# A delta rule in chunks of 128 tokens instead of 64, with one state hand-over, an output norm moved forward and a router product turned round

## The chip, the cores and the metric

The kernel runs on one core of a Trainium2 chip. The metric is the time of one execution in device microseconds. The kernel before took 1208.31 us in the median of 3 runs (1206.81 to 1208.69).

## What is computed

One block of a model with 256 tokens of width 1024. A mixer has two halves: a gated delta rule with 4 heads of 128 (the part that is changed) and a banded attention with 8 heads of 64. Behind it follow an output projection, a router that picks 4 of 32 experts for each token, and the experts. Of the reference, the delta rule per chunk of tokens is:

```python
lower = einsum(k_beta, k) * decay * strict           # chunk x chunk, below the diagonal
tmat  = inverse(lower + eye)                         # triangular
u = tmat @ (v * beta);  w = tmat @ (k_beta * exp(g))
attn = einsum(q, k) * decay;  q_dec = q * exp(g);  k_dec = k * exp(g_last - g)
def step(state, ...):                                # chunk after chunk
    v_new = u - w @ state
    out   = q_dec @ state + attn @ v_new
    state = state * exp(g_last) + k_dec.T @ v_new
```

The reference takes chunks of 64 tokens, so 4 chunks. The result does not depend on the chunk length: with chunks of 128 there are 2 chunks, the first state is zero, and only one state is ever handed on.

The router computes logits = x @ w_router + b_router, takes the 4 largest, and the experts (1024 to 2048 to 1024, in fp32) are run in the order of their load. All 32 experts are read: 192 blocks of 2 MB.

## The kernel before, in words

**Memory.** Eight blocks of 16 KB per partition (`w0`, `w1`, `wA` to `wF`, line 65) and two more slots (`wh`, `wx`) are first weights and scratch of the mixer and later the ring in which expert weights are loaded (`RINGTAGS`, line 23). An expert load (line 1109, issued by SyncE, SP in the rows) waits until the mixer's last use of its slot. In the mixer `wE` and `wB` are the scratch of the delta rule, `w0` is the scratch of the attention and then free, and `wF` takes one block of adaLN weights after another (line 81, `modrow`, line 717: five of the later ones on VectorE, the others on TensorE).

**Order.** Lines 62 to 1036 are not run in written order: a planner places each instruction in its engine's queue (the DMA queue of SP too) by costs of its own, and work under `tc.high_priority()` goes first. `chain()` (line 487) is run under high priority (line 848), so the planner fills the gaps of the delta rule with products of `stream()` (line 407, all `mm3` at line 232), `attention()` (line 746) and `wout_b()` (line 816, the attention's half of the output projection). Lines 1037 to 1080 are a stretch in which TensorE and VectorE keep the written order: `wout_a` (the delta rule's half of the output projection), the residual, the router, the first gather.

**The delta rule, lines 524 to 712.** Tokens lie in two tiles `a` of 128, each with two chunks `e` of 64; a chunk takes 64 partitions.

- Lines 524 to 533: products of k with k and q for each chunk (line 531, 64 x 64 x 128).
- Lines 535 to 554: sums of the gates by matrices `tri` and `same` (lines 537 to 541) and their exponentials, among them the decay `egl` of each state.
- Lines 557 to 588: decay matrices `xL`, `xA` of 64 x 64 for 8 pairs (tile, head), and `L` = lower.
- Lines 592 to 654: the triangular inverse `U` by six levels of doubling. `pair_mm` (line 597) makes 16 products of 64 x 64 x 64, half of them on partitions 0 to 63 and half on 64 to 127. Each level has `xb`, `ub` and, but for the last, `tb`.
- Lines 659 to 675: u (line 667) and w (line 673), 16 products each.
- Lines 678 to 712: four steps. Each has w @ state (line 688), k_dec.T @ v_new into the new state (line 696, with the scaled sum on VectorE at line 702) and the output (lines 707 and 708, 128-row and 64-row products by turns).

An fp32 product is two MATMUL instructions in the trace; a transpose is one.

**Behind it.** `delta_out(a)` (line 882) is the output norm of tile a with the gate: squares on ScalarE (line 886), eleven small steps and four products on VectorE, four transposes (line 893). `split(...)` at line 867 puts the high part of the first half of `w_out` into `whx` (tag `acc`, the place of `kqT`), so it waits for the delta rule's last use of q. `logits` (line 931) multiplies with x as the stationary side (128 x 128) and 32 columns of router weights moving, 8 products for each tile, before `choice` (line 939) on VectorE.

Of the kernel before, what the change touches and what calls it, by code (L numbers as in the profile page):

```python
# [19 lines left out]
NEG = -1e30  # L20
# [29 lines left out]
def block_kernel(ctx, tc, x, small, rows, rel_ext, wpre, wexp, b_up, b_down, out,  # L50
# [214 lines left out]
    def late_constants():  # L265
        nonlocal ones, same, tri, id64, m_strict, m_incT, lvl, iot, iou, strib, strif, onesb, kadd_r, kadd_c, ecol, e96
        ones = const.tile([P, P], F32, name="ones")
        G.memset(ones, 1.0)

        same = const.tile([P, P], F32, name="same")  # L270
        G.memset(same, 0.0)
        G.memset(same[0:64, 0:64], 1.0)
        G.memset(same[64:128, 64:128], 1.0)
        tri = const.tile([P, P], F32, name="tri")
        V.scalar_tensor_tensor(tri, jp, 0.0, same, op0=ALU.is_ge, op1=ALU.mult)
# [6 lines left out]
        m_strict = const.tile([P, 64], F32, name="m_strict")  # L282
        V.tensor_scalar(m_strict, jl, 0.0, NEG, op0=ALU.is_ge, op1=ALU.mult)
        m_incT = const.tile([P, 64], F32, name="m_incT")
        V.tensor_scalar(m_incT, jl, 0.0, NEG, op0=ALU.is_lt, op1=ALU.mult)
# [29 lines left out]
        G.memset(onesb, 1.0)  # L315
        kadd_r = const.tile([96, NE], F32, name="kadd_r")
# [15 lines left out]
    ones = same = tri = id64 = m_strict = m_incT = lvl = iot = iou = strib = strif = onesb = None  # L332
    kadd_r = kadd_c = ecol = e96 = None
# [13 lines left out]
    vT, eq, kw, vbt = [fixed["wB"][0][:, 1024 * i:1024 * i + 1024].rearrange("p (h t) -> p h t", h=n_)  # L347
                       for i, n_ in enumerate((4, 4, 8, 8))]
# [138 lines left out]
    def chain():  # L487
# [36 lines left out]
        mps = []  # L524
        for a in range(2):
            mp = bank("dl")
            mv = mp.rearrange("p (h z t) -> p h z t", h=4, z=2)
            for h in range(4):
                for e in range(2):
                    c0 = a * 128 + e * 64  # L530
                    T.matmul(mv[64 * e:64 * e + 64, h], kqT[:, h, 0, c0:c0 + 64], kqT[:, h, :, c0:c0 + 64],
                             start=True, stop=True)
            mps.append(mp)
        yield 0.6
        sp = bank("dl")
        for a in range(2):
            T.matmul(sp[:, 4 * a:4 * a + 4], tri, g[:, a, :], start=True, stop=True)
            T.matmul(sp[:, 8 + 4 * a:12 + 4 * a], same, g[:, a, :], start=True, stop=True)
            for e in range(2):
                c_ = 16 + (2 * a + e) * 4  # L540
                T.matmul(sp[:, c_:c_ + 4], same[:, 64 * e:64 * e + 1].to_broadcast([P, P]), g[:, a, :],
                         start=True, stop=True)
        V.tensor_scalar(ln_, ln_, -0.5, None, op0=ALU.mult)
        aL, bb, aq, kd, ew = [const.tile([P, 8], F32, name=n_) for n_ in ("aL", "bb", "aq", "kd", "ew")]
# [3 lines left out]
        V.tensor_add(kd, bb, sp[:, 8:16])  # L548
        egl = const.tile([P, 4, 4], F32, name="egl")
        S.activation(ew, aL, AF.Exp)  # L550
        S.activation(kd, kd, AF.Exp)
        S.activation(egl.rearrange("p c h -> p (c h)"), sp[:, 16:32], AF.Exp)
        betaf = beta.rearrange("p a h -> p (a h)")
        V.tensor_mul(ew, ew, betaf)
        yield 0.8

        blE = block("wE")
        xL, xA, L, Ti, *Xs, aT, U = [blE[:, 512 * i:512 * i + 512].rearrange("p (c n) -> p c n", c=8) for i in range(8)]

        for a in range(2):  # L560
            mv = mps[a].rearrange("p (h z t) -> p h z t", h=4, z=2)
            S.copy(L[:, 4 * a:4 * a + 4, :], mv[:, :, 0, :])
            S.copy(aT[:, 4 * a:4 * a + 4, :], mv[:, :, 1, :])
        for a in range(2):
            bp = bank("dl")
            for h in range(4):
                T.transpose(bp[:, h * 128:(h + 1) * 128], bb[:, a * 4 + h:a * 4 + h + 1].to_broadcast([P, P]), ident)
            bpv = bp.rearrange("p (h t) -> p h t", h=4)
            for e in range(2):
                r_ = slice(64 * e, 64 * e + 64)  # L570
                V.tensor_add(xL[r_, 4 * a:4 * a + 4, :], bpv[r_, :, r_], m_strict[r_, None, :].to_broadcast([64, 4, 64]))
        V.tensor_add(xL, xL, aL[:, :, None].to_broadcast([P, 8, 64]))
        S.activation(xL, xL, AF.Exp)
        yield 0.6
        for a in range(2):
# [3 lines left out]
            apv = ap_.rearrange("p (h t) -> p h t", h=4)  # L579
            if a == 0:  # L580
                G.tensor_mul(xL, xL, betaf[:, :, None].to_broadcast([P, 8, 64]))
            S.activation(eq[:, :, a * 128:(a + 1) * 128], apv, AF.Exp)
            for e in range(2):
                r_ = slice(64 * e, 64 * e + 64)
                V.tensor_add(xA[r_, 4 * a:4 * a + 4, :], apv[r_, :, r_], m_incT[r_, None, :].to_broadcast([64, 4, 64]))
        yield 1.5
        for a in range(2):
            V.tensor_mul(L[:, 4 * a:4 * a + 4, :], L[:, 4 * a:4 * a + 4, :], xL[:, 4 * a:4 * a + 4, :])
        idb = id64[:, None, :].to_broadcast([P, 8, 64])
        H0, H1 = slice(0, 64), slice(64, 128)  # L590

        def level(s_):
            lm = k2("Lm", (P, 8, 64))
            (V if s_ < 2 else G).tensor_mul(lm, L, lvl[s_][:, None, :].to_broadcast([P, 8, 64]))
# [84 lines left out]
        for c in range(4):  # L679
# [30 lines left out]
            if c < 3:  # L710
                st = sn
# [684 lines left out]
```

## Time and profile before

| what | value |
|---|---|
| median of 3 runs | 1208.31 us (1206.81 to 1208.69) |
| the profiled execution | 1208.93 us, its span in the trace 1207.2 us |
| TensorE busy / VectorE / ScalarE / GpSimdE | 87% / 30% / 16% / 8% of the span |
| mean granted TensorE clock | 0.945 of 2.4 GHz |
| read from memory | 449.5 MB, of them 402.7 MB expert weights |

The profile has two stages. Up to about 270 us the mixer and the router run; from then on the experts. 1.73 us of the execution's time lie outside the span. A row of the timeline names start, length, engine, line, operation, result and operands (out<-in), the count of merged instructions, and in brackets the idle time ahead and who ended it.

### The profile page before, as it was taken

To read this page: it belongs to the slowest core of one execution; us is meant where nothing else is said; L and a number is where in the kernel's file an instruction comes from. 1 tells how busy PE (TensorE), PEld (TensorE's weight loads), DVE (VectorE), ACT (ScalarE), POOL (GpSimd) and SP (SyncE) were. 2 spreads that over 40 slices of the span, in tenths; PEclk is the share of its full clock that TensorE was granted. 3 is DMA by queue.
4 is the path that set the end of the run, shared out by engine and by line. 5 is a ranking of instruction groups with operands and counts; after the bars stand their busy time and mean duration, and the time that the engine had idled before them with its cause. 6 is when DMAs were issued, how large, how long until landed. Compare 5 with 4: busy or idle time off the path is not lost. (4 is left out here: it accounts for less than half of the span.)

```text
span 1207.2 us, 14829 instructions
## 1 busy us (share of the span) xinstructions
PE 1055.9 (87%) x5891; PEld 508.5 (42%) x5891; DVE 361.0 (30%) x852; ACT 190.2 (16%) x380; POOL 102.3 (8%) x93
## 2 busy tenths in 40 slices
PE   4799999999987889999985889999976699998995
PEld 2698997673431124334431233334421143333332
DVE  5488786763113012121211012122211011111113
ACT  3554115331100001010100001010100001010101
POOL 1547413200000000000000000000000000000001
PEclk9899798989998799999997899999998799999998
DMA  9925345697999999999999999999999999999994
GB/s 356 400 78 210 140 176 210 259 426 280 423 420 422 421 407 422 426 425 423 426 420 426 426 423 427 423 427 427 419 428 422 425 428 422 426 426 422 427 420 162
DMA packets 51464, 451.95 MB, mean 374 GB/s; under 512 B 5760, under 2 KB 7424, under 8 KB 9408
## 3 DMA queue, kind: packets, MB, share of 16 engines
q1 hardware_dynamic: 51392, 450.97, 90.1%
q8 instruction: 48, 0.79, 0.3%
q14 instruction: 24, 0.20, 0.0%
HBM read 449.50 MB, written 1.05 MB: 373 GB/s over the span
## 5 line engine op out<-in xcount | busy, mean ns | idle before, releaser
L1117 PE MATMUL dl<-w_f,xg 128*64 128x512 f32 (+1 forms) x224 | 110.7, 638 | 9.1 <-DMA w_f<-in_wexp_dram 9.1
L1171 DVE TENSOR_TENSOR acc<-acc,mm 128x512 f32<-128x512 f32 x52 | 35.8, 688 | 248.2 <-PE mm L1166 248.2
L1117 PE MATMUL mm<-w_f,xg 128*64 128x512 f32 (+2 forms) x208 | 93.9, 602 | 3.0 <-DMA w_f<-in_wexp_dram 3.0
L1273 POOL TENSOR_TENSOR wF_f<-acc,m_row 128x512 f32<-128x512 f32 x3 | 3.8, 1284 | 944.4 <-DVE acc L1171 944.4
L1117 PE MATMUL dl<-wh,xg 128*64 128x512 f32 (+2 forms) x144 | 68.4, 617 | 4.9 <-DMA wh<-in_wexp_dram 4.9
L1117 PE MATMUL dl<-wD_f,xg 128*64 128x512 f32 (+1 forms) x128 | 62.5, 638 | 4.4 <-DMA wD_f<-in_wexp_dram 4.4
L1166 PE MATMUL mm<-yg,wts 128*128 128x512 f32 x112 | 54.5, 614 | 9.9 <-ACT yg L1163 8.9
L1135 ACT ACTIVATE sg<-gm 128x512 f32<-128x512 f32 x28 | 17.6, 630 | 279.8 <-DVE gm L1133 255.5
L1117 PE MATMUL dl<-wE_f,xg 128*64 128x512 f32 (+2 forms) x112 | 53.0, 623 | 7.9 <-DMA wE_f<-in_wexp_dram 7.9
L1117 PE MATMUL mm<-wB_f,xg 128*64 128x512 f32 (+2 forms) x128 | 59.2, 609 | 0.0
L1117 PE MATMUL mm<-wh,xg 128*64 128x512 f32 (+1 forms) x144 | 56.8, 594 | 0.0
L998 PEld LDWEIGHTS tp<-oh,x 128*128 128x128 f32 x432 | 50.7, 192 | 13.2 <-issue 11.4
L1117 PE MATMUL dl<-wF_f,xg 128*64 128x512 f32 (+2 forms) x112 | 53.7, 620 | 2.3 <-DMA wF_f<-in_wexp_dram 2.3
L998 PE MATMUL tp<-oh,x 128*128 128x128 f32 x432 | 54.8, 279 | 0.7 <-ACT aT__3409 L1146 0.7
L1117 PE MATMUL dl<-wC_f,xg 128*64 128x512 f32 (+2 forms) x112 | 53.1, 616 | 1.8 <-DMA wC_f<-in_wexp_dram 1.8
L1117 PE MATMUL mm<-wE_f,xg 128*64 128x512 f32 (+1 forms) x112 | 51.3, 611 | 2.5 <-DMA wE_f<-in_wexp_dram 2.5
L1163 ACT COPY yg<-dl 128x512 f32<-128x512 f32 x27 | 15.8, 586 | 228.6 <-PE dl L1117 228.6
L1117 PE MATMUL mm<-wC_f,xg 128*64 128x512 f32 (+1 forms) x112 | 51.6, 611 | 0.0
L1008 DVE TENSOR_SCALAR xg<-tp,mc,mc 128x128 f32<-128x128 f32 x52 | 19.6, 406 | 103.4 <-PE dl L1117 94.7
L1117 PE MATMUL dl<-wB_f,xg 128*32 128x512 f32 (+1 forms) x96 | 46.8, 625 | 2.8 <-DMA wB_f<-in_wexp_dram 2.8
L1006 ACT ACTIVATE xg<-tp,mc,mc 128x128 f32<-128x128 f32 x52 | 21.9, 455 | 147.6 <-DVE xg L1008 147.6
L1117 PEld LDWEIGHTS mm<-w_f,xg 128*64 128x64 f32 (+2 forms) x208 | 28.0, 139 | 37.9 <-issue 32.1
(633 smaller groups left out, 2236.8 us busy)
## 6 DMA issues: line engine op xcount, KB each, us to landing
wh<-in_wexp_dram SPq DMA_DIRECT2D x57, 1024.0 KB, 25.0
w_f<-in_wexp_dram SPq DMA_DIRECT2D x26, 2048.0 KB, 26.0
wA_f<-in_wexp_dram SPq DMA_DIRECT2D x36, 1024.0 KB, 22.2
wF_f<-in_wexp_dram SPq DMA_DIRECT2D x36, 1024.0 KB, 29.7
wE_f<-in_wexp_dram SPq DMA_DIRECT2D x15, 2048.0 KB, 29.4
wC_f<-in_wexp_dram SPq DMA_DIRECT2D x15, 2048.0 KB, 27.0
wB_f<-in_wexp_dram SPq DMA_DIRECT2D x13, 2048.0 KB, 22.2
wD_f<-in_wexp_dram SPq DMA_DIRECT2D x13, 2048.0 KB, 34.2
```

The costliest lines, as they stand in the source:

```text
L998: T.matmul(b_[:, k * 128:(k + 1) * 128], x2[:, a, half(n)][:, k * 128:(k + 1) * 128], oh[:, a], start=a == tiles[0], stop=a == tiles[-1])
L1006: S.activation(xg[:, k], src, AF.Identity, scale=mc, bias=sc)
L1008: V.tensor_scalar(xg[:, k], src, mc, sc, op0=ALU.mult, op1=ALU.add)
L1117: T.matmul(b_[i * n:(i + 1) * n, :], lhs[:, k, i * n:(i + 1) * n], w(k), start=k == 0, stop=last and k == 7)
L1135: S.activation(sg, gm, AF.Sigmoid, scale=1.702)
L1163: S.copy(yg, b_)
L1166: T.matmul(cb, wt[:, a], yg, start=True, stop=True)
L1171: V.tensor_add(acc[:, a, sl], acc[:, a, sl], cb)
L1273: (V if a and n else G).tensor_mul(fin[:, 0, a, sl], acc[:, a, sl], m3_row[:, sl])
```

## The change

The chunk becomes 128 tokens, a whole tile. Products of k and q, decay matrices and `L` are 128 x 128 for each pair (tile, head). The inverse is still made for the 64 x 64 blocks on the diagonal (`Ld`, the same levels), and the block below the diagonal comes from one coupling step of 2 x 8 products of 64 x 64 x 64 with a copy behind each. u, w and the outputs are products of 128 x 128 x 128, and one state goes from tile 0 to tile 1; `egl` and the decayed sum of states go. PSUM copies of this part are cut in two, one half for ScalarE and one for VectorE. Beside it: `delta_out(0)` stands under high priority; `whx` is taken from block `w0` instead of tag `acc`; the router's product has 32 router columns as the stationary side in four column groups and 128 tokens moving, then a copy and one product with `stk` (four stacked 32 x 32 identities) that adds the four groups and turns the result. The diff, cut:

```diff
-        V.scalar_tensor_tensor(tri, jp, 0.0, same, op0=ALU.is_ge, op1=ALU.mult)
+        V.tensor_scalar(tri, jp, 0.0, None, op0=ALU.is_ge)
...
+        for i in range(4):
+            V.tensor_copy(stk[32 * i:32 * i + 32], ident[32 * i:32 * i + 32, 32 * i:32 * i + 32])
...
+        def products(z, a):
+            mp = bank("dl")
+            for h in range(4):
+                T.matmul(mp[:, h * 128:(h + 1) * 128], kqT[:, h, 0, a * 128:(a + 1) * 128], kqT[:, h, z, a * 128:(a + 1) * 128],
+                         start=True, stop=True)
+            mv = mp.rearrange("p (h t) -> p h t", h=4)
+            if z == 0:
+                V.tensor_mul(L[:, 4 * a:4 * a + 4], mv, betaf[:, 4 * a:4 * a + 4, None].to_broadcast([P, 4, P]))
+            else:
+                S.copy(aT[:, 4 * a:4 * a + 4], mv)
...
-            T.matmul(sp[:, 8 + 4 * a:12 + 4 * a], same, g[:, a, :], start=True, stop=True)
-            for e in range(2):
-                c_ = 16 + (2 * a + e) * 4
-                T.matmul(sp[:, c_:c_ + 4], same[:, 64 * e:64 * e + 1].to_broadcast([P, P]), g[:, a, :],
+        T.matmul(sp[:, 8:12], ones, g[:, 0, :], start=True, stop=True)
...
+            for h in range(4):
+                c_ = 4 * a + h
+                V.scalar_tensor_tensor(xL[:, c_], bp[:, h * 128:(h + 1) * 128], aL[:, c_:c_ + 1], m_strict, op0=ALU.add, op1=ALU.add)
+            S.activation(xL[:, 4 * a:4 * a + 4], xL[:, 4 * a:4 * a + 4], AF.Exp)
...
+        for r_ in (H0, H1):
+            V.tensor_mul(Ld[r_], L[r_, :, r_], xL[r_, :, r_])
+        G.tensor_mul(L[H1, :, H0], L[H1, :, H0], xL[H1, :, H0])
...
+            else:
+                tb = pair_mm(X, Ti)[0]
+                V.tensor_sub(Ti[H0], Ti[H0], tb[H0])
...
+        for c_ in range(8):
+            T.matmul(xb[H0, c_], L[H1, c_, H0], U[H1, c_, H1], start=True, stop=True)
+        both(X[H0], xb, 1.0, H0)
+        for c_ in range(8):
+            T.matmul(ub[H0, c_], Ti[H0, c_, :], X[H0, c_, :], start=True, stop=True)
+        both(U[H0, :, H1], ub, -1.0, H0)
...
-        for c in range(4):
...
+        ub = heads()
+        for h in range(4):
+            T.matmul(ub[:, h], U[:, h], vbt[:, h], start=True, stop=True)
+        evac(u, ub)
+        wb = heads()
+        for h in range(4):
+            T.matmul(wb[:, h], kw[:, h], U[:, 4 + h], start=True, stop=True)
+        evac(wT, wb, -1.0)
+        ub = heads()
+        for h in range(4):
+            T.matmul(ub[:, h], U[:, 4 + h], vbt[:, 4 + h], start=h == 0, stop=False)
+        sb = heads()
+        for h in range(4):
+            T.matmul(sb[:, h], kdt[:, h], u[:, h], start=True, stop=True)
+        evac(st, sb)
+        ob = heads()
+        for h in range(4):
+            T.matmul(ob[:, h], aT[:, h], u[:, h], start=True, stop=True)
+        S.copy(oa[0].rearrange("p (h d) -> p h d", h=4), ob)
+        for h in range(4):
+            T.matmul(ub[:, h], wT[:, h], st[:, h], start=False, stop=h == 3)
+        evac(vn, ub)
+        ob = heads()
+        for h in range(4):
+            T.matmul(ob[:, h], qd[:, h], st[:, h], start=h == 0, stop=False)
+        for h in range(4):
+            T.matmul(ob[:, h], aT[:, 4 + h], vn[:, h], start=False, stop=h == 3)
+        S.copy(oa[1].rearrange("p (h d) -> p h d", h=4), ob)
...
-    spa = [split(blk["wo"][n], kv=KW, extra=(mem.tile([P, 2048], F32R, tag="acc", name="whx") if n == 0 else None))
+    spa = [split(blk["wo"][n], kv=KW, extra=(fixed["w0"][1][:, 0:2048] if n == 0 else None)) for n in range(2)]
...
-            T.matmul(rts[a][:, 0:32], x2Ts[a, n][:, k * 128:(k + 1) * 128], wrs[:, 4 * n + k, :], start=n + k == 0, stop=n + k == 4)
+            T.matmul(rts[a][32 * k:32 * k + 32, 128:256], wrs[:, 4 * n + k, :], x2Ts[a, n][:, k * 128:(k + 1) * 128],
+                     start=n == 0, stop=n == 1)
+        if n:
+            lt = k1("lt")[:, 0:128]
+            S.copy(lt, rts[a][:, 128:256])
+            T.matmul(rts[a][:, 0:32], lt, stk, start=True, stop=True)
...
-    for a in range(2):
-        delta_out(a)
+    with tc.high_priority():
+        delta_out(0)
+    delta_out(1)
```

`both` and `evac` copy one half on ScalarE and one on VectorE. `U` and `vbt` lie in `wE` now, `Ld`, `Ti` and the two `X` in `wB`.

## Rows read from the trace of the kernel before

**Rows 1.** The page, part 2: DMA busy tenths in 40 slices of 30.2 us.
```profile
DMA  9925345697999999999999999999999999999994
```
**Rows 2.** Stretches: from:to, length, busy of PE, PEld, DVE, ACT, POOL, granted clock, DMA share, GB/s.
```profile
120.78:133.05 12.27, 12.27 (x105) 11.74 (x106) 7.18 (x10) 1.93 (x2) 5.72 (x5) 0.52 0.46 172
196.50:203.30 6.80, 6.74 (x37) 5.45 (x37) 2.66 (x5) 4.00 (x13) 4.49 (x4) 0.51 1.04 442
60.00:251.60 191.60, 186.41 (x1646) 162.57 (x1644) 143.17 (x275) 72.42 (x153) 75.50 (x57) 0.94 0.50 192
258.30:269.90 11.60, 11.54 (x67) 10.99 (x67) 9.54 (x46) 5.76 (x18) 0.00 (x0) 0.58 1.01 427
```
**Rows 3.** Stretches of 5 us at the start of the experts, same columns.
```profile
270.00:275.00 5.00, 5.00 (x24) 1.89 (x25) 2.69 (x11) 0.00 (x0) 0.00 (x0) 1.00 0.49 200
275.00:280.00 5.00, 5.00 (x22) 1.69 (x21) 0.00 (x0) 0.84 (x2) 0.00 (x0) 1.00 0.34 88
```
**Rows 4.** Timeline of the DMA queue SP: refills of ring slots (w_f is w0).
```profile
190.04 1.23 SPq L1109 DMA_DIRECT2D wA_f<-in_wexp_dram  x2
...
220.88 0.33 SPq L1109 DMA_DIRECT2D w_f<-in_wexp_dram  x1
...
231.36 1.19 SPq L1109 DMA_DIRECT2D wF_f<-in_wexp_dram  x2
```
**Rows 5.** Groups of PE and DVE instructions by line and shape, 62 to 240 us.
```profile
L531 PE MATMUL dl<-kqT 128*64 128x128 f32 x32 | 2.9, 288 | 0.0
L641 DVE TENSOR_TENSOR wE_f<-wE_f,dl 64x512 f32<-64x512 f32 x10 | 6.8, 685 | 0.7 <-PE dl L601 0.3
```
**Rows 6.** Timeline of PE: gate sums and the row behind them, products of the inverse.
```profile
86.51 0.28 PE L537 MATMUL dl<-g,tri 128*128 128x4 f32 x2
...
88.22 0.72 PE L232 MATMUL mm<-wA_r,whx 128*128 128x256 f32 x4
...
120.78 3.51 PE L601 MATMUL dl<-wE_f 64*64 64x64 f32 x48 [1.88 <-DVE wE_f L635]
...
149.20 1.14 PE L601 MATMUL dl<-wE_f 64*64 64x64 f32 x16
...
157.58 1.15 PE L601 MATMUL dl<-wE_f,Lm 64*64 64x64 f32 x32
```
**Rows 7.** Timeline of PE: u, w, the steps of the state, the end of `wout_a(1, 0)`.
```profile
186.25 1.96 PE L667 MATMUL dl<-wB_f,wE_f 64*64 64x128 f32 x24
...
190.01 2.73 PE L673 MATMUL dl<-wE_f,wB_f 64*128 64x64 f32 x29
...
196.56 1.96 PE L708 MATMUL dl<-wE_f 64*64 64x128 f32 x8 [1.91 <-ACT wE_f L674]
...
215.66 1.16 PE L696 MATMUL dl<-vn,kdt 64*128 64x128 f32 x8
216.75 0.43 PE L707 MATMUL dl<-wE_f,kqT 128*64 128x128 f32 x2
...
219.63 1.09 PE L801 MATMUL mm<-w_f,wC_f 128*64 128x128 f32 x14
220.56 1.04 PE L688 MATMUL dl<-wE_f 128*64 128x128 f32 x8
221.43 0.38 PE L707 MATMUL dl<-wE_f,kqT 128*64 128x128 f32 x2
...
247.66 1.09 PE L232 MATMUL mm<-wD_r,wC_r 128*128 128x512 f32 x4
```
**Rows 8.** Timeline of PE: a later gather, fp32 products of 128 x 128 x 128.
```profile
303.55 3.84 PE L998 MATMUL tp<-oh,x 128*128 128x128 f32 x32
```
**Rows 9.** Timeline of ACT: the cast ahead of w's copy.
```profile
194.12 1.90 ACT L217 CAST wh<-w_f 128x2048 fp32r<-128x2048 f32 x1 [3.25 <-DMA w_f<-in_wpre_dram]
```
**Rows 10.** Timeline of PE: a product in four column groups, and the router's, second tile.
```profile
100.89 1.92 PE L196 MATMUL tp<-wB_f,csil 128*32 128x512 f32 x16
...
260.32 3.60 PE L935 MATMUL mm<-wrs,x2T 128*128 128x32 f32 x16
```

More of the change, by code (lines that the diff above doesn't have):

```diff
@@ L330, in late_constants @@
             V.tensor_scalar(e96[32 * i:32 * i + 32], jp[32 * i:32 * i + 32, 0:1], -1.0, -32.0 * i, op0=ALU.mult, op1=ALU.add)
-    ones = same = tri = id64 = m_strict = m_incT = lvl = iot = iou = strib = strif = onesb = None
-    kadd_r = kadd_c = ecol = e96 = None
+    ones = tri = id64 = m_strict = m_incT = lvl = iot = iou = strib = strif = onesb = None
+    kadd_r = kadd_c = ecol = e96 = stk = None
     late_constants()
@@ L346, in block_kernel @@
     ws["kb"] = hload(7, "w1")
-    vT, eq, kw, vbt = [fixed["wB"][0][:, 1024 * i:1024 * i + 1024].rearrange("p (h t) -> p h t", h=n_)
-                       for i, n_ in enumerate((4, 4, 8, 8))]
+    blB = block("wB")
+    vT = blB[:, 0:1024].rearrange("p (h t) -> p h t", h=4)
+    eq, kw = [blB[:, 1024 + 512 * i:1536 + 512 * i].rearrange("p (h t) -> p h t", h=4) for i in range(2)]
     def conv(part, h, b_):
@@ new lines, in chain, with both @@
+        qd = kqT[:, :, 1, 128:256]
+        def both(dst, src, scale, r_):
+            S.mul(dst[:, 0:4], src[r_, 0:4], scale)
+            V.tensor_scalar(dst[:, 4:8], src[r_, 4:8], scale, None, op0=ALU.mult)
+        X = Xs[0]
+        xb, ub = [bank("dl").rearrange("p (c n) -> p c n", c=8) for _ in range(2)]
+        for c_ in range(8):
[3 more added lines that the diff above has]
+            T.matmul(ub[H0, c_], Ti[H0, c_, :], X[H0, c_, :], start=True, stop=True)
@@ new lines, in chain, with heads, evac @@
+        both(U[H0, :, H1], ub, -1.0, H0)
+        yield 0.6
+        u = blE[:, 0:512].rearrange("p (h d) -> p h d", h=4)
+        st = blE[:, 512:1024].rearrange("p (h d) -> p h d", h=4)
+        vn = k2("vn", (P, 4, 128))
+        blk["oa"] = oa = [blE[:, 3072 + 512 * i:3584 + 512 * i] for i in range(2)]
+        def heads():
+            return bank("dl").rearrange("p (h d) -> p h d", h=4)
+        def evac(dst, src, scale=None):
+            for eng, sl in ((S, slice(0, 2)), (V, slice(2, 4))):
+                if scale:
+                    (S.mul if eng is S else lambda o, i, c_: V.tensor_scalar(o, i, c_, None, op0=ALU.mult))(dst[:, sl], src[:, sl], scale)
+                else:
+                    (S.copy if eng is S else V.tensor_copy)(dst[:, sl], src[:, sl])
```

146 lines of the change are left out of this document (34 added, 112 removed).

## The prediction

> **What bounds the kernel now.** I read the page first. Its DMA line [rows 1] shows two stages: from the ninth slice on, about 240 us, the DMA engines are full but for one slice, so the expert stage is bound by reading weights. Such a stage ends a fixed time after it begins. The stage table shows where it begins: between 270 and 280 us the DMA engines are only 49% and 34% busy [rows 3]. There all ring slots are full, and the loads wait for the first expert products to free one. So the end of the kernel is set by the time at which the mixer and the router are done, with a reserve of DMA time of 0.51 x 5 + 0.66 x 5 = 5.9 us that a faster front would not need.
>
> The front itself is bound by TensorE: from 60 to 251.6 us it is busy 186.41 of 191.60 us, VectorE 143.17, ScalarE 72.42 [rows 2]. The reader should see that the planner has filled nearly every gap of the delta rule with products of the projections and the attention. Work taken from TensorE there comes off the time; a shorter chain alone would not. The timeline of PE then shows two waits of 1.9 us in this stretch, at 120.78 behind VectorE's copy of a level [rows 6] and at 196.56 behind w's copy on ScalarE [rows 7]. After each, the granted clock is 0.52 for 12.27 us and 0.51 for 6.80 us, which is the level of 1.2 GHz [rows 2]. Half of such a stretch is lost: 6.1 and 3.4 us.
>
> **The change, part by part, on TensorE.** One fp32 product of 128 x 128 x 128 is two instructions of 3.84 / 32 = 0.12 us [rows 8].
> - Products of k with k and q: 32 instructions in 2.9 us go [rows 5], 32 of 0.12 come: +0.9.
> - Gate sums: 16 instructions between 86.51 and 88.22, so 1.71 us, 0.107 each [rows 6]; six stay: -1.1.
> - A last `tb` of 32 instructions: 1.15 us when both halves run together [rows 6]: +1.15. Run apart, one half has 16 in 1.14 [rows 6], so 2.3 is the upper end.
> - Coupling: 16 products on one half of the partitions, 32 instructions at 1.14 for 16 [rows 6]: +2.3. Between and behind them stand copies, priced below.
> - Tail, out: u 32 x 1.96 / 24 = 2.6; w 32 x 2.73 / 29 = 3.0; the products into the state three times 216.75 - 215.66 = 1.09, so 3.3; w @ state three times 221.43 - 220.56 = 0.87, so 2.6; the outputs three times 219.63 - 216.75 = 2.88, so 8.6, and 1.96 for the first [rows 7]. Together 22.1 us. In: 32 products, 64 instructions of 0.12, 7.7 us. -14.4.
>
> The sum is 0.9 - 1.1 + 1.15 + 2.3 - 14.4 = -11.1 us. The largest term is the outputs: 128-row and 64-row products by turns take 0.18 us each there, against 0.12 for a whole one.
>
> The pairs on the two halves are what the change gives up. The rows show a clear gain from pairs in the inverse (32 instructions in 1.15 us against 16 in 1.14 for one half alone), and a smaller one for u, 82 ns each against the 60 ns that half of 0.12 would be [rows 6 to 8]. The Trainium skill (TensorEngine Tiling (Array Packing), section Theoretical Speedup) says that a dimension of 64 or less may be packed for up to twice the speed, which speaks against this change. By that rule u, w and the products of k would have cost 32 x 60 ns = 1.9 us each before, 2.8 less than I take out, and the sum would be -8.3; I go by the rows.
>
> **Other engines.** VectorE: 10 operations of 512 columns go (lines 572, 647, 669, 675, 690, a third of `ktv`) and 5 come; 22 narrower ones go and 22 come. At 0.685 us a wide one [rows 5] this is -3.4 us of 143, covered by TensorE's queue; without that cover it would be a small gain. ScalarE and GpSimd change by less than 1 us each: the second exponential and the wider multiplication of `aT` stand against copies of half the length. Constants (`same`, `stk`, masks) are made before 60 us beside the projection of k. The `k1` buffers that `lt` takes push `cmp_` onto the place of the first one-hot matrix; the planner may put it behind the gather, and what it feeds is needed only at the end of the first expert products. I cost these at nothing.
>
> **The waits.** The wait at 196.56 goes with its instruction, the first output: 1.91 and 3.4 us, less about 1.0 that is in the tail's sum already, so up to 4.3 us more. Its cause need not go. ScalarE ran a 1.9 us cast of `w_out` that had itself waited 3.25 us for its DMA [rows 9], and w's copy stood behind it. The new tail has seven hand-overs from TensorE to copies and back (two of the coupling, u, the state, v_new, two outputs), and nearly all have a half on ScalarE. So I bound the waits between -4.3 (none in the tail) and +1.9 + 3.4 = 5.3 for one like the old one beyond it, and take -1, since one of the old kind is as likely as not.
>
> **Steps that are moved.** `delta_out(0)` issues four squares on ScalarE, eleven small steps and four narrow products on VectorE, four transposes, a cast and a subtraction. They now go ahead of the casts and copies of the attention's output projection on ScalarE and of adaLN weights on VectorE; who waits for these is work that TensorE needs only behind 250 us or in later groups. Hidden by the filler: 0. If the cover is gone, the second tile's norm alone lies ahead of `wout_a` in either kernel. `whx` in `w0` is no longer held by q, but the refill of `w0`, issued at 220.88 [rows 4], must now wait until the first column half of `wout_a` is through, at 247.66 in the times of before [rows 7]. Its 2.1 MB then fall into the full stretch: 2.1 MB / 427 GB/s = 4.9 us at the rate of the stretch behind 258 us [rows 2], out of the reserve of 5.9. What remains, 1.0 us, is all that a faster router could give.
>
> **The router.** 16 instructions took 3.60 us for the second tile [rows 10], whose stretch was granted 0.58 [rows 2]. The new form has four column groups; the nearest row is 16 instructions of 512 columns in 1.92 us [rows 10], so between 0.5 (a quarter of the columns) and 1.9 for the products, twice that at 1.2 GHz, then a copy on ScalarE between 0.3 and 0.6 and two instructions of 0.12 to 0.24, with TensorE's queue standing still during the copy. Second tile: 1.0 + 0.6 + 0.5 = 2.1 at best, 3.8 + 1.1 at worst, against 3.6. I take 0, between -1.0 (the reserve) and +1.3.
>
> **The sum.** -11.1 - 1 + 0 = -12.1 us on the profiled execution's 1208.93 (its span 1207.2 and 1.7 around it), so 1196.8; this execution stands 0.6 above the median, so about 1196.5.
>
> **The rivals.**
> 1. Forecast: TensorE's work comes off and the waits stay about as they are. For it: the front is 97% TensorE. 1192 to 1201. Chance 0.50.
> 2. Neither of the two stretches at 1.2 GHz comes back: a further 1.9 + 6.1 = 8.0 us for the one at 120.78, so 1188. The new VectorE load is lighter, but the copy of each level stays behind other work on VectorE as before. 0.12.
> 3. The tail's hand-overs find no filler and add a stretch at 1.2 GHz: 5.3 us back, 1202, with bounds 1201 to 1206. For it: the tail is now a chain of short steps and the planner's costs missed the wait at 196.56. 0.20.
> 4. The gain does not reach the experts. The refill of `wF` at 231.36 [rows 4] opens the full stretch; it hangs on adaLN weights that pass through one buffer, VectorE and TensorE. If it does not move, the loads end no sooner, and only 5.9 - 4.9 = 1.0 us is left: 1207.5. Against it: that buffer's last products are filler on the same TensorE queue. 0.07.
> 5. Slower, by the order of SP's queue. If the planner leaves the refill of `w0` ahead of `wF`, `wh`, `w1`, `wB` and `wE`, these stand behind a wait until 247.7 - 12 = 236 us. The full stretch then begins 236 - 231 = 5 us later and has 4.9 us more to carry: 5 + 4.9 - 5.9 = 4, so 1212.5. The point from which it decides is an issue of `w0` that stands before `wF`'s and is later than 231 + 1.0 us. Against it: `wA`, which is behind `w0` in ring order, was issued before it, at 190.04 [rows 4], so the planner orders by time of release. 0.11.
>
> That the early norm does nothing is part of every case, since I give it 0. The Trainium skill (TensorE: Matmul & The Clock Gate, section Loop structure matters more than you think) puts the clock down to how the loops keep the engine fed. By it the new tail's small steps would bring rival 3; the rows agree so far as both stretches at 1.2 GHz follow a wait.
>
> **How the numbers follow.** The time is that of case 1, 1196.5. The range takes case 1, case 3 and most of case 2: 1187 to 1206, chance 0.8. About 0.2%, 2.4 us, is what a measurement of this kernel can tell from no change. Faster by more: cases 1 to 3, 0.82. Within it: case 4, 0.07. Slower: case 5, 0.11.
>
> **What would show it.** Right: the rows of u, state and output add up to some 8 us on TensorE instead of 22; the first expert product starts about 12 us sooner, near 258; the DMA share of the ten microseconds behind it is near full, not 0.4; the refill of `w0` is issued near 236. Wrong: TensorE idle in the tail with a granted clock near 0.5 behind it (case 3); a first product at 258 that waits for DMA (case 4); `w0` ahead of `wF` in SP's queue with an idle DMA behind it (case 5); or products of 128 x 128 x 128 that take other than 0.12 us there.

## The result, and the profile after

The changed kernel takes 1192.39 us in the median of 4 runs (1191.11 to 1194.84), the kernel before on the same chip 1208.5 (1206.81 to 1208.88). The ratio is 0.9872, 95% interval 0.9853 to 0.989: 16 us less. The profiled execution took 1192.22 us, its span is 1190.4 us.

I read the profile of the changed kernel in the order of the prediction. First the DMA line of the page, in the same 40 slices as [rows 1] (a slice is 29.8 us here).

```profile
DMA  9925346989999999999999999999999999999993
```

The two stages are still there, and the full stretch begins about one slice sooner. Then the timeline of PE, for the start of the experts: the last products of `wout_a`, the first transposes behind the residual, the second tile of the router, the gather that follows it, the first expert product.

```profile
234.78 1.07 PE L232 MATMUL mm<-wD_r,wC_r 128*128 128x512 f32 x4
...
236.60 1.29 PE L925 MATMUL tp<-ident,x 128*128 128x128 f32 x8 [0.76 <-DVE x L917]
...
244.81 1.46 PE L935 MATMUL mm<-x2T,wrs 128*32 128x128 f32 x16
246.65 0.64 PE L940 MATMUL mm<-stk,lt 128*128 128x32 f32 x2 [0.39 <-ACT lt L939]
247.10 2.05 PE L1003 MATMUL mm<-oh,x 128*128 128x128 f32 x8
...
253.53 0.64 PE L1123 MATMUL mm<-wB_f,xg 128*64 128x512 f32 x1
```

The gather behind the router and the first expert product in the timeline of the kernel before:

```profile
263.74 2.05 PE L998 MATMUL mm<-oh,x 128*128 128x128 f32 x8
...
269.91 0.64 PE L1117 MATMUL mm<-wB_f,xg 128*64 128x512 f32 x1
```

`wout_a` ends at 235.85 instead of 251.54 in the timeline of before (its first column half ended at 248.75 [rows 7], here it ends at about 233.1). The first expert product starts at 253.53 instead of 269.91: 16.4 us sooner, and the span is 16.8 us shorter. So the whole gain is made in the front, and all of it reaches the end.

Next the stretches, with the columns of [rows 2]: the front from 60 us to the end of `wout_a`, the one long wait of it, the new tail, and the start of the experts.

```profile
60.00:235.80 175.80, 167.44 (x1599) 151.43 (x1597) 141.24 (x271) 72.66 (x152) 78.59 (x59) 0.96 0.54 206
114.00:123.50 9.50, 7.11 (x58) 6.84 (x58) 9.30 (x9) 2.31 (x3) 8.81 (x6) 0.64 0.41 171
180.90:205.00 24.10, 23.17 (x207) 19.77 (x205) 18.34 (x39) 16.07 (x44) 13.61 (x11) 1.00 0.66 262
255.00:265.00 10.00, 10.00 (x46) 3.37 (x44) 1.32 (x5) 0.84 (x2) 0.00 (x0) 1.00 0.57 213
```

TensorE is busy 167.44 us of the front instead of 186.41 [rows 2], 19.0 less, and idle 8.4 instead of 5.2. The tail runs at full clock: it is busy for 23.17 of 24.10 us, where the kernel before had a wait of 1.91 us and 6.80 us at 1.2 GHz [rows 2, 7]. The rows of the tail:

```profile
188.25 1.06 PE L684 MATMUL dl<-wE_f 128*128 128x128 f32 x8
189.24 1.09 PE L800 MATMUL mm<-w_f,wC_f 128*64 128x128 f32 x14
...
190.75 1.06 PE L688 MATMUL dl<-wE_f,wB_f 128*128 128x128 f32 x8
191.64 1.06 PE L692 MATMUL dl<-wE_f 128*128 128x128 f32 x8
193.63 1.16 PE L696 MATMUL dl<-wE_f,kdt 128*128 128x128 f32 x8 [0.93 <-DVE wE_f L680]
...
198.59 1.16 PE L700 MATMUL dl<-wE_f 128*128 128x128 f32 x8
199.58 1.06 PE L703 MATMUL dl<-wE_f,kdt 128*128 128x128 f32 x8
```

A group of eight instructions starts 0.89 us ahead of the next group (190.75 to 191.64), so one takes 0.11 us. Between the steps stand products of the attention (L800) and of the projections, and only one of the seven hand-overs leaves TensorE waiting, for 0.93 us.

The other wait, in the inverse, is still there and is longer. The timeline of PE:

```profile
116.39 2.69 PE L595 MATMUL dl<-wE_f,Lm 64*64 64x64 f32 x32 [3.73 <-DVE wE_f L621]
```

The timeline of VectorE (DVE) of the changed kernel, ahead of that step and behind it:

```profile
113.04 2.71 DVE L725 SCALAR_TENSOR_TENSOR wF_f<-wF_f,csil 128x512 f32<-128x512 f32 x1
115.67 1.39 DVE L621 TENSOR_TENSOR wE_f<-id,dl 64x512 f32<-64x512 f32 x2
...
118.64 4.72 DVE L725 SCALAR_TENSOR_TENSOR wF_f<-wF_f,csil 128x512 f32<-128x512 f32 x3
```

And the timeline of VectorE of the kernel before, at the wait of [rows 6]:

```profile
115.17 4.83 DVE L726 SCALAR_TENSOR_TENSOR wF_f<-wF_f,csil 128x512 f32<-128x512 f32 x3
120.03 0.69 DVE L635 COPY wE_f<-dl 64x512 f32<-64x512 f32 x1
```

In both kernels an adaLN block on VectorE (L726 before, L725 after) stands ahead of the step of the inverse that TensorE waits for. The wait is 3.73 us now and was 1.88. Behind it 5.6 us at 1.2 GHz follow (to 122.0 us); in the kernel before the granted clock stayed at that level up to 134.9 us, beyond the 133.05 of [rows 2], so for 13.7 us. With half of the low stretch as lost, the event costs 6.5 us now and cost 8.7.

### The profile page after: what moved, and what is told of

It reads as the page before. It is cut to its first block, busy times and chain, and to the rows that moved or that the text cites. A ratio compares the mean times of both kernels' runs of the same rounds, so it can differ in the third digit from the quotient of the medians.

```text
span 1190.4 us, 14727 instructions
## 1 busy us (share of the span) xinstructions
PE 1029.8 (87%) x5845; PEld 495.3 (42%) x5845; DVE 358.7 (30%) x851; ACT 190.3 (16%) x380; POOL 104.1 (9%) x91
## 5 line engine op out<-in xcount | busy, mean ns | idle before, releaser
L1123 PE MATMUL dl<-w_f,xg 128*64 128x512 f32 (+1 forms) x224 | 113.5, 653 | 9.7 <-DMA w_f<-in_wexp_dram 9.7
L1279 POOL TENSOR_TENSOR wF_f<-acc,m_row 128x512 f32<-128x512 f32 x3 | 3.8, 1273 | 943.1 <-DMA w_f<-in_wexp_dram 937.3
L1123 PE MATMUL dl<-wD_f,xg 128*64 128x512 f32 (+1 forms) x128 | 65.4, 662 | 4.3 <-DMA wD_f<-in_wexp_dram 4.3
L1169 ACT COPY yg<-dl 128x512 f32<-128x512 f32 x27 | 15.8, 585 | 224.8 <-PE dl L1123 224.8
L1123 PEld LDWEIGHTS dl<-w_f,xg 128*64 128x64 f32 (+1 forms) x224 | 28.2, 134 | 42.6 <-issue 25.7
L1139 DVE TENSOR_SCALAR gm<-dl 128x512 f32<-128x512 f32 x14 | 9.7, 692 | 119.5 <-PE dl L1134 119.5
```

The costliest lines, as they stand in the source:

```text
L1123: T.matmul(b_[i * n:(i + 1) * n, :], lhs[:, k, i * n:(i + 1) * n], w(k), start=k == 0, stop=last and k == 7)
L1139: V.tensor_scalar(gm, bs[0], 7.0, None, op0=ALU.min)
L1169: S.copy(yg, b_)
L1279: (V if a and n else G).tensor_mul(fin[:, 0, a, sl], acc[:, a, sl], m3_row[:, sl])
```

## The experiments

Each kernel was run beside the kernel before on the same chip, and the kernels of one batch share these runs. Executions of the kernel before lie further apart (1199.9 to 1215.6 us over all batches) than the four of the changed one (1191.1 to 1194.8), so its median moved between 1205.85 and 1208.5.

### The small parts without the longer chunk

The kernel before with the early norm of the first tile, `whx` in `w0`, and the router's product turned round:

```diff
+            T.matmul(rts[a][32 * k:32 * k + 32, 128:256], wrs[:, 4 * n + k, :], x2Ts[a, n][:, k * 128:(k + 1) * 128],
...
+    with tc.high_priority():
+        delta_out(0)
```

> The kernel before with the three smaller parts of the change alone: the early norm of tile 0, the high part of w_out in w0, the turned router product; the delta rule stays in chunks of 64. Theory: all but about 1 us of the 16 us comes from the delta rule's rewrite, so this gives 1207 to 1208.5. Rival: the three parts and the new order that they bring to the planner are worth 4 us or more, 1204 or less.

1206.52 us (1200.74 to 1211.67, 12 runs) against 1205.85: ratio 1.0004 (0.9987 to 1.0021). Without the chunk nothing is gained. Its profiled execution is its shortest, 1200.74 us with a span of 1198.9. Timeline of PE at the place of the wait of [rows 6]:

```profile
118.28 1.20 PE L604 MATMUL dl<-wE_f 64*64 64x64 f32 x20
119.85 1.14 PE L604 MATMUL dl<-wE_f 64*64 64x64 f32 x28 [0.37 <-DVE wE_f L644]
```

And its stretch there, with the columns of [rows 2]:

```profile
118.00:134.00 16.00, 14.76 (x209) 13.60 (x208) 11.43 (x17) 5.03 (x5) 13.01 (x10) 1.00 0.43 162
```

Here TensorE had products of a projection until VectorE's copy was done, only a wait of 0.37 us was left, and the clock stayed at 1.00 where [rows 2] shows 0.52. Its first expert product is at 261.68, 8.2 us ahead of the profile of before. That is near the 8.0 us of rival 2 for the wait of 1.88 us and the low stretch behind it, though other stretches at 1.2 GHz differ as well (behind w's copy 3.4 us instead of 6.8, about the router 13.7 instead of 10.2). It may be why executions of one program differ, but only one execution of each program has a trace. The kernel before agrees so far as its seven executions below 1202 us were granted a mean clock of 0.953 to 0.963, its profiled one 0.945.

### Undo the router, `whx` or the priority

Three kernels, each the changed one with one part as before:

```diff
-            T.matmul(rts[a][32 * k:32 * k + 32, 128:256], wrs[:, 4 * n + k, :], x2Ts[a, n][:, k * 128:(k + 1) * 128],
...
+            T.matmul(rts[a][:, 0:32], x2Ts[a, n][:, k * 128:(k + 1) * 128], wrs[:, 4 * n + k, :], start=n + k == 0, stop=n + k == 4)
```

> The changed kernel with the router's product as it was; the front up to the residual has the same instructions in the same order. Theory: the turned product gives the second tile about 1.1 us (from its first product to the gather 3.4 us before, 2.3 after), and as the loads still wait for the first expert products at the start of the experts, this reaches the end: 1193.5 us, 1.1 above the changed kernel. Rival: the copy and the extra product eat it, the router's form is worth nothing: 1192.4, within 0.5.

1192.76 us, ratio 0.9892 (0.9871 to 0.9913): the same within what can be told. In the trace the old form costs 1.3 us more: from the first transpose behind the residual (L925) to the first expert product it takes 256.54 - 238.34 = 18.2 us, in the changed kernel 253.53 - 236.60 = 16.9. The rest of its later start, 1.7 us, arose earlier in that execution's front; it was the longest of the five, 1195.8 us.

```diff
-    spa = [split(..., extra=(fixed["w0"][1][:, 0:2048] if n == 0 else None)) for n in range(2)]
+    spa = [split(..., extra=(mem.tile([P, 2048], F32R, tag="acc", name="whx") if n == 0 else None)) for n in range(2)]
```

> The changed kernel with the high part of w_out back in the place of q, so that the refill of w0 is free early again. Theory: the late refill of w0 is paid from the idle DMA time at the start of the experts; undoing it changes the end by less than 1 us, and the idle DMA time there grows by about 4.9 us from the 4.4 of the changed kernel. Rival: the late refill does cost; undoing it gives 2 us or more, 1190 or less.

1191.44 us, ratio 0.9882 (0.9858 to 0.9905), again the same. The refill of `w0` goes out at 205.43 instead of 232.31, but the DMA engines' idle time at the start of the experts is 4.8 us, not 4.9 us more than the changed kernel's 4.3. The front also came out 2.0 us sooner here (251.53), so this run alone doesn't give the price of the late refill; the pair further down does.

```diff
-    with tc.high_priority():
-        delta_out(0)
-    delta_out(1)
+    for a in range(2):
+        delta_out(a)
```

> The changed kernel without the high priority of the first tile's norm. Every engine's queue holds the same instructions in the same order as in the changed kernel, so every theory expects the same time, 1192.4 within 1 us; what differs is what a repeat differs by.

1192.38 us, ratio 0.989 (0.9864 to 0.9917). The planner gives every engine the same order of instructions with and without the priority, so this part of the change does nothing at all. The run is also a second measurement of the changed kernel, and gives 13.5 us on another chip.

### The old outputs, with their two shapes apart

```diff
+            if st is not None:
+                for h in range(4):
+                    T.matmul(ob[r_, h * 128:(h + 1) * 128], qd[:, h, c * 64:c * 64 + 64], st[:, h, :], start=h == 0, stop=False)
             for h in range(4):
-                if st is not None:
-                    T.matmul(ob[r_, h * 128:(h + 1) * 128], qd[:, h, c * 64:c * 64 + 64], st[:, h, :], start=True, stop=False)
                 T.matmul(ob[r_, h * 128:(h + 1) * 128], aT[r_, 4 * a + h, :], vn[:, h, :], ...)
```

> The kernel before, in which each of the three outputs with a state issues its four products with q (128 rows) first and then its four with the chunk's vn (64 rows), instead of the two kinds by turns. The same 48 instructions. Theory (the prediction's largest term, 0.18 us per instruction, is the price of changing shape at every product, and the front is bound by TensorE): an output takes 16 instructions of about 0.11 and 0.08, so 1.5 us instead of 2.88; three of them save 4.1 us, and the time falls by 2 to 5 us, a third of what the whole change gave, without any longer chunk. Rival A (the 0.18 us belong to products of 64 rows or to the place in the queue, whatever the order): 0.17 to 0.19 us stay, and the time stays within 1.5 us. Rival B (the outputs are cheaper, but the chain of waits, not the work, sets the end of the front): 0.11 or less per instruction, and a time within 1.5 us.

1198.03 us (1196.79 to 1207.35, 12 runs) against 1207.75: ratio 0.9937 (0.9906 to 0.9968). The timeline of PE of this kernel, one output and the row behind it:

```profile
205.39 1.09 PE L707 MATMUL dl<-wE_f,kqT 128*64 128x128 f32 x8
206.40 1.08 PE L709 MATMUL dl<-vn,wE_f 64*64 64x128 f32 x8
207.42 0.66 PE L787 MATMUL tp<-ident,w_f 128*128 128x128 f32 x4
```

16 instructions take 2.03 us, 0.127 each, where by turns they took 2.88 [rows 7]. So the price of changing shape is real, 0.85 us an output and 2.6 in all, less than the 4.1 that I expected. The profiled execution agrees: its first expert product is at 267.17, 2.7 us sooner than before, with the same low stretches in its front. The times fell by more, 4 to 11 us by the interval. Rivals A and B both fall. Why the median moved by more than the work isn't shown; nine of its 12 executions lie between 1196.8 and 1200.2 and three above 1203, the profiled one (1206.2) among these. The six below 1198 us were granted a mean clock of 0.954 to 0.961, the other six 0.946 to 0.950, so less time at 1.2 GHz is part of it; which stretch was missing is not shown.

The Trainium skill (TensorEngine Tiling (Array Packing), section Tiling Modes) says that changing the tiling mode drains TensorE. The trace agrees so far as sorting by shape takes the price away: with a change after every two instructions two take 0.36 us, without it 0.25, so 0.11 us for each change.

### Work that nothing needs

The changed kernel with unused products ahead of the attention:

```diff
+    for _ in range(12):
+        xtra = bank("tp")
+        for h in range(4):
+            T.matmul(xtra[:, h * 128:(h + 1) * 128], ones, tri, start=True, stop=True)
```

> The changed kernel with work added that nothing uses: 48 products of 128 x 128 x 128 of two constants on TensorE, 96 instructions of some 0.115 us, 11 us, which are free to be placed in any gap of the delta rule. Theory (the front is still bound by TensorE's work after the change): the first expert product moves from 253.5 to about 264.5 us and the time rises by 8 to 12 us, to 1200 to 1204. Rival (after the change the delta rule's chain of hand-overs is the bound, and TensorE has room): the work falls into gaps, TensorE's idle time between 60 us and the end of the output projection (8.4 us) shrinks by most of 11 us, and the time rises by less than 3 us.

1212.05 us, ratio to before 1.003 (1.0005 to 1.0056): 19.7 us above the changed kernel, more than either theory gave. Timeline of PE: the first row is the added work, the last a wait that the changed kernel doesn't have.

```profile
181.87 2.05 PE L865 MATMUL tp<-tri,ones 128*128 128x128 f32 x16
183.68 0.61 PE L232 MATMUL mm<-wh,wA_r 128*128 128x256 f32 x3
...
218.76 1.97 PE L800 MATMUL mm<-w_f,wC_f 128*64 128x128 f32 x16 [6.04 <-DVE wC_r L806]
```

16 instructions take 1.81 us, so 96 take 10.9. The first expert product moves by 19.8 us (273.36). What is above 10.9 is new waits: the planner put the unused products beside the inverse, and the attention came to stand behind it without cover, with this wait of 6.0 us and three of 2.8 us in all on GpSimdE, and a longer stretch at 1.2 GHz (213.5 to 223.8 us). The rival, that TensorE has room, is out. That work costs its own time and no more holds only where the order of the rest stays.

### The tail's copies whole on ScalarE

```diff
-            S.mul(dst[:, 0:4], src[r_, 0:4], scale)
-            V.tensor_scalar(dst[:, 4:8], src[r_, 4:8], scale, None, op0=ALU.mult)
+            S.mul(dst[:, 0:8], src[r_, 0:8], scale)
...
-            for eng, sl in ((S, slice(0, 2)), (V, slice(2, 4))):
+            for eng, sl in ((S, slice(0, 4)),):
```

> The changed kernel, in which the copies out of PSUM in the new tail and in the coupling are made whole on ScalarE instead of one half on ScalarE and one on VectorE. The same TensorE work; six hand-overs become longer by 0.3 to 0.6 us each, 2 to 4 us in all. Theory (the filler products hide the hand-overs): the time stays within 1.5 us, and the tail's granted clock stays near 1.0. Rival (the tail is bound by its hand-overs): the time rises by 3 us or more, with waits on ScalarE's copies in the tail and, if one of them is long enough, a stretch near 0.5 behind it.

1190.28 us, ratio 0.9855 (0.9801 to 0.9908), with the first expert product at 253.41, where the changed kernel has 253.53. The waits on its copies in the tail are 0.40 and 0.31 us. The time is as the theory had it, but the run doesn't test longer hand-overs: a whole copy takes 0.57 to 0.62 us where a half took 0.35 to 0.42, yet VectorE's halves came late in the changed kernel. The second copy of the coupling, for one, was done at 190.00 there and is done at 187.53 here. It does show that neither placement of the copies brings the waits of rival 3.

### One adaLN block on TensorE, in either kernel

The block whose products stand on VectorE ahead of the step that the inverse waits for is made on TensorE; the same edit was made in the changed kernel and in the kernel before:

```diff
-ADA = list("DDPDDPDD")
+ADA = list("DDPDPPDD")
```

> The changed kernel with one adaLN block (the one whose products with the condition stand on VectorE just ahead of the copy that the inverse waits for at 116.4 us, for 3.7 us) made on TensorE instead. TensorE gets 1.9 us of work more, VectorE some 4 to 6 us less. Theory (the wait of 3.7 us and the stretch at 1.2 GHz of 6.9 us behind it are one event, caused by what stands ahead of the copy on VectorE): the wait goes, 3.7 + 3.4 - 1.9 = 5 us come off at most, and the time falls by 2 to 5 us, to 1187 to 1190. Rival (the copies of the inverse are slow because GpSimdE is busy beside them, whatever stands ahead): the wait stays at 2 us or more with the low clock behind it, and the time rises by 0 to 2 us.

1192.76 us, ratio 0.9879 (0.9838 to 0.992). The wait at 116 us and its low stretch are gone, and another wait of the inverse takes their place, again behind VectorE (timeline of PE):

```profile
150.35 1.14 PE L595 MATMUL dl<-wB_f 64*64 64x64 f32 x16 [2.13 <-DVE wE_f L633]
```

The stretch behind it:

```profile
150.35:155.00 4.65, 4.64 (x35) 4.58 (x36) 4.52 (x8) 0.78 (x2) 0.00 (x0) 0.68 0.00 0
```

The theory's wait went, but the time is the rival's, not to be told from the changed kernel's; the rival's cause, GpSimdE busy beside the copies, isn't there, as GpSimdE (POOL) ran nothing from 138.2 to 161.5 us. The first expert product is 0.7 us sooner: what the wait gave, the added work and the new waits took.

> The kernel before, with the same one adaLN block made on TensorE instead of VectorE (its three products with the condition, 1.6 us each, stand ahead of the copy that the inverse waits for at 120.78 us). Chunks of 64 as before. Theory (the wait of 1.88 us and the stretch of 12.27 us at 1.2 GHz behind it are one event of VectorE's queue, and have nothing to do with the chunk length): the wait and the low stretch at 120 us go, 1.9 + 6.1 - 1.9 (added work) = 6 us come off an execution that has them, and the time falls by 3 to 7 us with a smaller spread between executions. Rival (the low clock comes from the small products of the inverse themselves): the stretch stays or comes at another place of the inverse, and the time moves by less than 2 us or rises.

1210.93 us, ratio 1.0041 (1.0018 to 1.0065): 5 us slower. The stretch at 120 us is gone, as the theory said, but the time goes the other way. A wait of 1.32 us ahead of 130.34, again behind VectorE, is followed by a new stretch, and another stands in the steps of the state, behind a wait of 0.64 us at 212. Its stretches:

```profile
130.00:137.00 7.00, 6.66 (x45) 6.54 (x46) 4.74 (x7) 0.95 (x2) 3.32 (x4) 0.52 0.43 137
214.00:222.00 8.00, 8.00 (x27) 4.52 (x25) 3.31 (x16) 0.58 (x1) 0.00 (x0) 0.58 0.97 412
```

By the letter this is the rival's forecast: the stretch came at another place of the inverse, and the time rose. Its cause doesn't hold, since the small products of the inverse run at a granted clock of 1.00 where no such wait stands ahead of them (in the changed kernel from 122 to 181 us). So the wait at 120 us comes from VectorE's queue with either chunk length, but it is not one that an edit takes out alone: the filler moves, and the next step that VectorE is late with becomes the wait.

### Parts that did no harm, put together

> The changed kernel with three parts together: the high part of w_out back on its own slot, the tail's copies whole on ScalarE, the one adaLN block on TensorE. Each alone was within 2 us of the changed kernel, with a first expert product 2.0, 0.1 and 0.7 us sooner. If they add up: 1188.5 to 1190.5 us. If only one of them can show, because DMA idle time at the start of the experts (4.4 us in the changed kernel) is used up or a new wait takes its place: 1190.5 to 1192.5.

> As a_combo1, with a second adaLN block (the next one on VectorE beside the inverse) on TensorE too: 1.9 us of TensorE work more. If waits in the inverse behind VectorE still cost more than that (the run with one block had 2.13 us at 150 us and a low stretch of 3 us behind it): 1187 to 1190. If not: 1 to 2 us above a_combo1.

> The changed kernel with the high part of w_out back on its own slot and the tail's copies whole on ScalarE; the adaLN blocks stay where the change has them. TensorE's work is the same as in the changed kernel. If the first expert product is all that counts: 2.0 + 0.1 us sooner than 253.5, and 1190 to 1191. If the two add up to more, since the refill of w0 leaves the full DMA stretch: 1188 to 1190. If the placement falls out worse, as with two adaLN blocks on TensorE: above 1192.5.

The first takes 1191.06 us, ratio 0.9877 (0.9835 to 0.9918), with a first expert product 1.7 us sooner (251.85) and not 2.8: it doesn't add up. The second takes 1202.56, ratio 0.998 (0.9955 to 1.0006), 11 us above the first for one more block on TensorE, which neither of its two cases had. Its timeline of PE shows TensorE idle ahead of a product of adaLN weights, with no releaser in the profile, so the cause stays open:

```profile
227.36 1.84 PE L728 MATMUL tp<-ones,wB_f 128*128 128x1 f32 x8 [7.43 <-issue]
```

The third takes 1190.12 us (1189.32 to 1191.98), ratio 0.985 (0.9823 to 0.9877). It is the lowest of all, but its interval overlaps that of the changed kernel, so it is not shown to be faster, and its first expert product is not 2.1 us sooner but at 253.55: the 2.0 us of the kernel with `whx` back alone did not come again. It has its use as a pair with the kernel of the section on ScalarE, from which it differs only in the place of `whx`. Stretches of that one:

```profile
205.00:215.00 10.00, 9.15 (x51) 7.49 (x50) 9.86 (x16) 5.43 (x13) 3.51 (x2) 1.00 0.77 271
255.00:265.00 10.00, 10.00 (x46) 3.40 (x45) 1.23 (x4) 0.84 (x2) 0.00 (x0) 1.00 0.61 229
```

The same stretches of this one:

```profile
205.00:215.00 10.00, 8.44 (x47) 6.54 (x46) 9.96 (x17) 4.73 (x12) 3.85 (x3) 1.00 1.00 393
255.00:265.00 10.00, 10.00 (x46) 3.39 (x44) 1.34 (x6) 0.84 (x2) 0.00 (x0) 1.00 0.34 114
```

With the early refill of `w0` the DMA engines are full at 205 to 215 us and idle 6.6 us at the start of the experts; with the late one they are idle 2.3 and 3.9 us. The late refill takes 2.7 us of the reserve; about the rest of its 4.9 us is the 2.3 us in which the DMA engines are idle earlier. First expert products (253.41 and 253.55) and spans (1190.5 and 1190.1) are alike: whether 3.9 or 6.6 us are idle there makes no difference to the end.

## Why the prediction was right, and where its terms were off

**The end follows the first expert product.** The span less the time of that product is 937.3 us in the kernel before, 936.9 in the changed one, and between 936.4 and 937.9 in all 14 kernels, with first products from 251.5 to 273.4 us. Whatever moves the front moves the end by as much; rival 4 is out. The point was forecast 12 us sooner, near 258, and came 16.4 us sooner, so that the time lies at the low end of the forecast's case 1 (1192 to 1201). (The last step of the sum is off: 1208.93 less 12.1 and 0.6 is 1196.2, not 1196.5.)

**TensorE's work: -13.4 us instead of -10.1.** I multiplied the busy time of each stretch of 2 us from 60 us to the end of `wout_a` by its granted clock, and summed: 175.0 us at full clock before, 161.6 after. On this scale the forecast's -11.1 is -10.1, since its 22.1 us for the old tail hold 1.0 us that the first output lost at 1.2 GHz. By the lines, each instruction taken from its start to the start of the next one and at full clock:
- The tail was right: from 20.9 to 7.8 us, -13.1, where the forecast without that 1.0 is -13.4. With the two shapes by turns alone, 2.6 us of it could have been had in the old chunks; the rest is fewer and fuller products.
- The coupling was right: 0.9 and 1.2 us, 2.1 against 2.3. So were the products of k, from 2.5 to 3.3 us, +0.8 against +0.9, and the gate sums, from 1.7 to 0.6 us, -1.1 as forecast. The groups, whose busy time is larger because it counts the last product of a run to its end, beside which the next one has started:

```profile
L595 PE MATMUL dl<-wB_f 64*64 64x64 f32 x320 | 16.0, 221 | 0.3 <-DVE wB_f L627 0.3
...
L532 PE MATMUL dl<-kqT 128*128 128x128 f32 x32 | 4.4, 278 | 0.0
L662 PE MATMUL dl<-wB_f 64*64 64x64 f32 x16 | 1.4, 224 | 0.0
...
L659 PE MATMUL dl<-wE_f 64*64 64x64 f32 x16 | 1.1, 221 | 0.0
```

- The term that was mis-sized is the inverse. "A last `tb` of 32 instructions: +1.15" stands there, and the other 480 instructions are left at their old price. But the inverse as a whole went from 23.6 to 21.9 us, -1.7, with 512 instructions instead of 480: 43 ns each instead of 49. Two halves that run beside each other take 36 ns an instruction and one half alone 71 [rows 6], so more of the products found their partner. In the timeline of PE of the kernel before, eight groups of the inverse are 16 instructions of one half alone, seven of them in its first two and its last level; in the changed kernel there is one such group. Why the halves came together is not shown; no run here keeps the chunk and changes only that.

The rule of the Trainium skill that I had set against the rows (TensorEngine Tiling (Array Packing), section Theoretical Speedup) gave -8.3; the measurement decides for the rows. Halves got their double speed in the inverse (36 against 71 ns), but not in u, w and the products of k, which took 2.9, 2.8 and 2.5 us before and not 1.9 each.

**The waits: -2.4 us, where the forecast on this scale is -2.0** (its -1, and the 1.0 of low clock from the tail). Idle time rose by 3.2 us and the loss by the clock fell from 11.5 to 5.9. That the sum came near is luck in good part, since its parts were others than I had. The wait at 196.56 went with its low stretch, 5.3 us, and the tail has a wait of 0.93 us in its place. The wait in the inverse, which I left as it was, grew by 1.9 us, but its low stretch is 5.6 us instead of 13.7. And a wait came that I had put at nothing, on the output norm, with 3.4 us at 1.2 GHz around it (220.98 to 224.39). Its products on VectorE and TensorE's transposes behind it:

```profile
217.91 3.22 DVE L888 SCALAR_TENSOR_TENSOR wE_f<-wE_f,rso,zg 128x128 f32<-128x128 f32 x4
221.26 1.97 PE L891 MATMUL tp<-ident,wE_f 128*128 128x128 f32 x8 [1.49 <-DVE mc L733]
```

The same four products in the kernel before:

```profile
234.96 1.14 DVE L890 SCALAR_TENSOR_TENSOR wE_f<-wE_f,rso,zg 128x128 f32<-128x128 f32 x4
```

Both waits stand behind VectorE steps that took long while GpSimdE worked (last section): these four beside steps of GpSimdE from 218.07 to 220.72 us, and the adaLN step at 113.04, 2.71 us, beside the product of `aT` with its decay (L645, 2.52 us, twice as wide as before, where it took 1.74). The wider product is a thing that the prediction priced at less than 1 us of GpSimdE alone. That it made the wait longer is read from the trace; no run takes it away. -13.4 - 2.4 gives the 15.8 us by which the front to the end of `wout_a` is shorter.

**The router: -0.8 us instead of 0.** From the first transpose behind the residual to the first expert product it is 17.7 us before and 16.9 after. The second tile's product to the gather takes 247.10 - 244.81 = 2.3 us instead of 3.4, near the 2.1 that I had as the best case. It is below what the times can tell.

**The refill of `w0`** went out at 232.31, where I had 236, behind `wF` at 216.32, so the order of SP's queue, rival 5, did not come up. The timeline of SP's queue:

```profile
216.32 1.19 SPq L1115 DMA_DIRECT2D wF_f<-in_wexp_dram  x2
...
232.31 0.33 SPq L1115 DMA_DIRECT2D w_f<-in_wexp_dram  x1
```

But its price was mis-sized: I took all 4.9 us of its transfer from the reserve, and the pair above shows 2.7, since in about half of the time that it leaves free earlier the DMA engines are busy with other loads. I expected a DMA share near full behind the first expert product; it is 0.57 over ten us, so 4.3 us of the reserve are left.

**What I put at nothing** was nothing in part: VectorE was busy 141.24 instead of 143.17 us, the priority of the first norm changes no queue, and but for 0.93 us the tail's hand-overs are hidden. The norm's products beside GpSimdE, and the wider product of `aT`, were not.

**The rivals.** Rival 3 did not happen: the tail's clock is 1.00 with its copies on two engines, and the run on ScalarE has no long wait there either. Rival 2 did not happen in the changed kernel, where the stretch in the inverse came back behind a longer wait. With the old chunk it is seen in one execution, the one above at 1200.74 us of the kernel without the chunk; against it the gain is some 8 us, not 16.

## What to carry to other kernels

Where one engine is full in a stage, count its instructions by their measured spacing in the very order in which they stand: products of two shapes by turns took 0.18 us, the same products sorted 0.127, and whole ones 0.11. Look for the one event that the rest of the kernel hangs on (here the first expert product, with 937 us behind it in every kernel) and price each part of a change by what it does to that. In a queue that a planner fills, an edit of 2 us may cost 11 or nothing, because the filler moves: measure the version, and don't add up what parts gave alone.

## What the runs showed of the hardware

- Steps on VectorE with both operands in SBUF took about twice their time or more while GpSimdE worked: three products of an adaLN block take 4.72 us at 118.64, 1.57 each, against 0.77 each at 124.12, when GpSimdE is idle. Two sums with one operand in PSUM, at 115.67 beside GpSimdE, take the usual 0.69 each. The Trainium skill (SBUF — State Buffer, section SBUF: two separate sides) calls the port pair of the two engines an exclusive lock: a VectorE step with two SBUF inputs and a GpSimdE step that reads SBUF block each other for the whole instruction. The trace agrees, the step of 2.71 us at 113.04 ending 0.6 us behind the end of a GpSimdE step that ran from 112.67 for 2.52 us. I had costed VectorE's steps at one price.
- Waits of 1.3 to 3.7 us in the inverse were followed by stretches at 1.2 GHz of 3 to 14 us, one of 0.37 us was not. The length of the wait alone doesn't tell: with one adaLN block moved in the kernel before, a stretch came behind a wait of 0.64 us in the steps of the state, and none behind 0.93 us in the new tail. The wait of 1.88 us at 120.78 with the half of the 13.7 us behind it that is lost makes 8.7 us, over four times its length.
